# Recurrence lanes that count as emitted 300 instructions earlier, in a one-layer hybrid encoder step

## The chip, the cores and the metric

The kernel runs on one core of a Trainium2 chip. The metric is the device time of one execution in microseconds (us); lower is better. PE is TensorE's matmul stream and PEld its weight loads, DVE is VectorE, ACT ScalarE, POOL GpSimd, SP SyncE, which here only issues DMAs.

## The reference

One layer of a streaming encoder, for a prompt of 2048 frames and a sample of 32 frames with running state, model width 1024. All inputs are float32.

```python
h = _rmsnorm(x, attn_norm_g[l])
(u_a, qkv_b, qkv_c, z_c, a_c, b_c, q_d, k_d, v_d, g_d, gk_d) = _split_cols(einsum('btd,dc->btc', h, w_in[l]))
y_a, st_pool = _pool_mixer(u_a, ...)                 # trailing means over 2/4/8/16 frames, a 64x64 product
y_b = _band_attention_prompt(q_b, k_b, v_b, rel_bias[l])   # 4 heads, own chunk of 64 and the 8 before it
y_c, st_conv, st_d = _delta_mixer(qkv_c, z_c, a_c, b_c, ...)  # gated DeltaNet, chunks of 64, a state per head
y_d, st_g = _gla_mixer(q_d, k_d, v_d, g_d, gk_d, ...)      # gated linear attention, chunks of 64, a state per head
x = x + einsum('btc,cd->btd', concatenate([y_a, y_b, y_c, y_d]), w_out[l])
h2 = _rmsnorm(x, mlp_norm_g[l])
x = x + einsum('btf,fd->btd', square(relu(einsum('btd,df->btf', h2, w_up[l]))), w_down[l])
y = _rmsnorm(x, final_norm_g)
```

In DeltaNet each chunk of 64 frames solves a triangular system and then updates a 64x64 state per head; the next chunk needs that state. GLA likewise carries a 32x64 state per head from chunk to chunk. Attention has no such chain, but each head goes through scores, softmax, transposes and the product with the values.

## The kernel before

**Two phases.** Phase 1 (`phase1`) makes the mixer: the input projection, the four head groups and the output projection. Phase 2 (`phase2`) is the MLP in three blocks of 696 or 688 frames. Projections are split into a high and a low float32r part, so that each product is three matmuls (line 90 is the one line from which every matmul is recorded; line 94 records PE transposes).

**Phase 1 as a fill and three lanes.** The prompt is cut into four blocks of 512 frames. The *fill* is a generator: for each block `stage_in` projects the normed input piece by piece (tiles g on PE, weights `wt` split from `ldt` at lines 252 and 253, the input `hT` split at 255 and 256 or, for the output projection, 252 and 253) and spills the results to DRAM; after the four blocks `out_proj` loads the mixed rows (`yt`, line 1360) and the old x (`sg<-x_t`, line 1377) and adds the output projection to x (line 1421). Three *lanes* run beside it: delta (tiles d, un, X, Sd; `delta_tile`), attention (s, pT, oa, nb, qkr; `attn_head`, `attn`) and GLA (l, att, Qx, Cl; `gla`). A lane loads what the fill has spilled (qkr at line 734, nb at 713, lqke and qz at 1049 and 1052, ltk at 1055, lg at 1162) and writes its part of the mix with `mix_out` (transposes a on PE, a copy mo on ACT at line 848, a store). Small *jobs* are run by `tick`: stores, the pooling mix (a<-sg,pv on PE, line 670 on ACT), the norm of the next block (lines 311 and 321), and `delta_pre`, which inverts the triangular factors by 31 steps of two DVE instructions (tp at line 999, X at 1000) and transposes (ut at 1005, tr at 1007, then U at 1027).

**What sets the order.** `drive` emits the program: one step of the fill, now and then a tick of the jobs, and then from each lane as many steps as its rate has earned. What it emits is numbered; the scheduler of the framework then orders each engine's instructions by list scheduling: it keeps all dependences, follows a model of how long instructions take, and where several are ready for an engine it takes the one with the lowest number. `high_priority(offset=n)` lowers the numbers of what is emitted inside by n; phase 2 uses it with 400 for reads of its accumulators. Two things bind the fill to the lanes beyond data: `pace` puts the fill's next matmul behind what each lane had emitted on PE seven steps earlier, and accumulators, buffers and DRAM tiles are shared through pools (two accumulators `a`, one of each lane's, four loads `ldt`/`yt`, six `sg`, one nb, three qkr). Each engine runs its queue in order, and SP issues its DMAs in order.

Of the kernel before, what the change touches and what calls it, by code (L numbers as in the profile page):

```python
# [110 lines left out]
class K:  # L111
# [1317 lines left out]
    def drive(self, fill, lanes):  # L1429


        state = [[list(l), 0.0, None, 0] for l in lanes]
        live = True
        tk = 0.0
        hist, seen = [], {}
        while live:
            hist.append(dict(self.front))
            if fill is not None and len(hist) > LAG:
                past = hist[len(hist) - 1 - LAG]
                self.bound = [x for l, x in past.items() if seen.get(l) is not x]  # L1440
                seen = past
            w = next(fill, None) if fill is not None else None
            if w is None:
                fill = None
            tk += 2.6 if w is None else w
            if tk > 2.0:
                tk = 0.0
                self.tick()
            live = False
            for self.lane, st in enumerate(state):  # L1450
                work = st[0]
                if not work:
                    continue
                live = True
                cond, g, rate, _ = work[0]
                if self.rest:
                    if st[2] is None:
                        st[2] = (sum(w[3] for w in work) - st[3]) / self.rest
                    rate = max(rate, st[2])
                if not cond():  # L1460
                    st[1] = min(st[1], 0.5)
                    continue
                st[1] += (2.6 if w is None else w) * rate
                while st[1] >= 1.0 and work:
                    st[1] -= 1.0
                    st[3] += 1
                    if next(g, g) is g:
                        work.pop(0)
                        st[3] = 0
                        if not work or not work[0][0]():  # L1470
                            break
                        g = work[0][1]
            self.lane = None
        self.bound = []
# [490 lines left out]
```

## Time and profile before

| What | Before |
|---|---|
| device time, median of 3 runs | 2712.63 us (2703.66 to 2714.59) |
| the profiled execution: its own time, its span | 2714.24 us, 2712.5 us |
| PE, PEld busy | 2594.9 us (96%), 2415.3 us (89%) |
| DVE, ACT, POOL busy | 1962.2 us (72%), 1079.0 us (40%), 872.9 us (32%) |
| mean granted clock of TensorE | 0.98 |
| from 200 to 1300 us: PE, PEld, DVE busy | 1039.47, 890.66 and 820.24 of 1100 us |

The span reaches from the first to the last instruction of the profiled execution. PE's matmuls are pipelined and their ends are modelled, so a busy PE need not be at its peak. Phase 1 ends at about 1290 us. The granted clock is the share of 2.4 GHz; it has two levels, 1.0 and 0.5.

### The profile page before, as it was taken

The page shows a single profiled execution, that of the slowest core. Times are in us where ns is not written, and L with a number is a line of the kernel's source. Part 1 is how long each engine was busy: PE and PEld are TensorE (multiplying, and loading weights), DVE is VectorE, ACT ScalarE, POOL GpSimd, SP SyncE. Part 2 cuts the span into 40 slices and gives each one's busy share as a digit, 9 for nine tenths or more (in the row PEclk, how much of TensorE's full clock was granted, in tenths as well). Part 3 has the DMA queues.
Part 4 walks back from the last instruction along what each step waited for, and adds up shares of the span by engine and source line. Part 5 has one row for each costly group of instructions (what it writes and reads, how often), then busy time and mean ns, then how long its engine had stood idle before and what let it go on. Part 6 is the DMA issues. An engine that isn't in the chain of part 4 may idle for free.

```text
span 2712.5 us, 44728 instructions
## 1 busy us (share of the span) xinstructions
PE 2594.9 (96%) x17012; PEld 2415.3 (89%) x17012; DVE 1962.2 (72%) x3498; ACT 1079.0 (40%) x1934; POOL 872.9 (32%) x1064
## 2 busy tenths in 40 slices
PE   7899998999899999998999999999999999999998
PEld 7787787788778877878999999999999999999998
DVE  6567779878887865566787667778766677767665
ACT  6435643653465443343433223443232343333232
POOL 4433564464446543322221112222212213211211
PEclk9998999999999999999999999999999999999999
DMA  5655454454545566366353222455322235222221
GB/s 165 175 152 162 124 179 146 129 159 137 150 139 162 158 185 195 103 209 205 105 180 114 70 71 78 139 161 171 111 70 86 75 108 160 80 70 79 71 70 50
DMA packets 229144, 349.21 MB, mean 129 GB/s; under 512 B 52032, under 2 KB 152784, under 8 KB 228928
## 3 DMA queue, kind: packets, MB, share of 16 engines
q1 hardware_dynamic: 162384, 295.49, 36.1%
q10 hardware_dynamic: 66480, 50.78, 5.7%
q8 instruction: 134, 2.20, 0.3%
q14 instruction: 82, 0.67, 0.1%
q0 software_dynamic: 64, 0.08, 0.0%
HBM read 273.83 MB, written 73.56 MB: 128 GB/s over the span
## 4 chain that ended last, share of the span: by engine, by line
PE 47%; DVE 7%; DMA 4%; issue 2%; ACT 1%; POOL 1%; SPq 0%; DVEq 0%; ACTq 0%; POOLq 0%
PE d L90 23%; PE u L90 19%; PE g L90 3%; DVE wx L253 1%; DVE acc L1824 1%; DMA cbd<-cb 1%; DVE wt L253 1%; DMA ldt<-w_o 1%; DMA x2d<-sg 1%; DVE h2T L253 1%; DVE acc L1853 1%; DVE u L253 1%; PE l L90 0%; DMA cb<-cbd 0%; PE s L90 0%
## 5 line engine op out<-in xcount | busy, mean ns | idle before, releaser
L90 PE MATMUL d<-u,wt 128*128 128x348 f32 (+1 forms) x2400 | 629.9, 323 | 4.5 <-DVE acc L1824 3.7
L90 PE MATMUL d<-u,wx 128*128 128x348 f32 (+1 forms) x2208 | 600.6, 323 | 9.5 <-DVE acc L1824 9.4
L90 PE MATMUL g<-hT,wt 128*128 128x512 f32 (+2 forms) x2544 | 544.2, 362 | 18.3 <-DVE sg L1421 7.1
L1824 DVE TENSOR_TENSOR acc<-acc,d 128x348 f32<-128x348 f32 (+1 forms) x752 | 376.0, 510 | 214.3 <-PE d L90 206.5
L90 PE MATMUL u<-h2T,wt 128*128 128x348 f32 (+1 forms) x2024 | 515.9, 323 | 6.5 <-DVE wt L253 6.2
L90 PE MATMUL u<-h2T,wx 128*128 128x348 f32 (+1 forms) x2008 | 514.0, 323 | 1.1 <-ACT wt L252 0.9
L90 PEld LDWEIGHTS g<-hT,wt 128*128 128x128 f32 x2544 | 414.4, 194 | 81.1 <-DVE hT L256 6.1
L90 PEld LDWEIGHTS d<-u,wt 128*128 128x128 f32 x2400 | 426.6, 189 | 7.5 <-DVE acc L1824 5.3
L90 PEld LDWEIGHTS d<-u,wx 128*128 128x128 f32 x2208 | 396.7, 189 | 13.9 <-DVE acc L1824 13.1
L90 PEld LDWEIGHTS u<-h2T,wt 128*128 128x128 f32 x2024 | 357.7, 189 | 8.9 <-DVE wt L253 7.4
L90 PEld LDWEIGHTS u<-h2T,wx 128*128 128x128 f32 x2008 | 356.6, 190 | 2.7 <-ACT wt L252 1.1
L1699 POOL TENSOR_TENSOR s<-wur 128x512 f32<-128x512 f32 x48 | 74.4, 1550 | 725.3 <-DMA wur<-w_up 603.7
L90 PE MATMUL g<-wt,hT 128*128 128x256 f32 (+3 forms) x1632 | 243.7, 298 | 6.7 <-DVE sg L464 3.1
L90 PEld LDWEIGHTS g<-wt,hT 128*128 128x128 f32 (+1 forms) x1632 | 214.3, 189 | 16.0 <-DVE sg L464 4.1
L253 DVE TENSOR_TENSOR wt<-ldt,wt 128x1024 fp32r<-128x1024 f32 (+1 forms) x120 | 163.4, 1361 | 70.2 <-ACT wt L252 69.4
L252 ACT CAST wt<-wur 128x1024 fp32r<-128x1024 f32 x126 | 131.4, 1049 | 184.9 <-PE u L90 119.3
L252 ACT CAST wx<-wur 128x1024 fp32r<-128x1024 f32 x114 | 118.8, 1049 | 200.7 <-PE u L90 144.9
L1780 ACT COPY k<-u 128x348 f32<-128x348 f32 (+1 forms) x144 | 64.0, 447 | 281.6 <-PE u L90 280.8
L253 DVE TENSOR_TENSOR wx<-wur,wt 128x1024 fp32r<-128x1024 f32 x125 | 158.7, 1269 | 19.5 <-PE d L90 8.4
L252 ACT CAST wt<-ldt 128x1024 fp32r<-128x1024 f32 (+1 forms) x120 | 126.0, 1050 | 115.9 <-PE g L90 78.3
L1699 POOL TENSOR_TENSOR wur<-s,wur 128x512 f32<-128x512 f32 x48 | 66.4, 1383 | 324.7 <-DVE wt L253 172.2
L253 DVE TENSOR_TENSOR wt<-wur,wx 128x1024 fp32r<-128x1024 f32 x114 | 146.2, 1285 | 24.7 <-PE d L90 8.4
(348 smaller groups left out, 3821.8 us busy)
## 6 DMA issues: line engine op xcount, KB each, us to landing
wur<-w_up SPq DMA_DIRECT2D x96, 512.0 KB, 3.7
wur<-w_down SPq DMA_DIRECT2D x96, 512.0 KB, 4.2
ldt<-w_fm SPq DMA_DIRECT2D x56, 512.0 KB, 4.4
ldt<-w_o SPq DMA_DIRECT2D x32, 512.0 KB, 4.9
ldt<-w_tm SPq DMA_DIRECT2D x24, 512.0 KB, 4.2
fmd<-sg ACTq DMA_DIRECT2D x46, 256.0 KB, 2.9
qkr<-fmd SPq DMA_DIRECT2D x88, 128.0 KB, 3.5
tmd<-sg ACTq DMA_DIRECT2D x64, 128.0 KB, 2.6
```

The costliest lines, as they stand in the source:

```text
L90: return self.order(self.k.nc.tensor.matmul(out, lhsT, rhs, start=not have, stop=True, skip_group_check=True))
L252: nc.scalar.copy(hi, src)
L253: (eng or nc.vector).tensor_tensor(lo, src, hi.bitcast(F32), ALU.subtract)
L1699: add = lambda o, x, y: nc.gpsimd.tensor_tensor(o, x, y, ALU.add)
L1780: nc.scalar.copy(keep[n], ps[z].t[:, :h])
L1824: nc.vector.tensor_tensor(x, x, ps.t[:, :cw], ALU.add)
L1853: nc.vector.scalar_tensor_tensor(x, x, self.fg[:, i:i + 1], fs[0], ALU.mult, ALU.mult)
```

## The change

In `drive`, the step of a lane is emitted inside `high_priority(offset=300)`. All that a lane emits (its matmuls, its DVE, ACT and POOL instructions and its loads) is numbered as if it had been emitted 300 instructions earlier; what the fill and the jobs emit keeps its number, the stores of `mix_out` among it, since `tick` emits them. No instruction is added or taken away, and buffers and dependences stay.

```diff
                 while st[1] >= 1.0 and work:
                     st[1] -= 1.0
                     st[3] += 1
-                    if next(g, g) is g:
+                    with self.tc.high_priority(offset=300):
+                        end = next(g, g) is g
+                    if end:
                         work.pop(0)
                         st[3] = 0
                         if not work or not work[0][0]():
```

The built programs show where instructions went. Three places follow, each with the rows of before first; the numbers in names are those of the tiles, the same in both programs.

ACT, in the third block of the input projection: mo_7983 and mo_7988 are copies of two lanes' transposes for the mix, U_8195 belongs to `delta_pre`, sg_8133 to sg_8141 to the norm of the next block, sg_7859 to the pooling mix. Before:

```order
L697 COPY pT_7909<-s_334_7812 128x640
L252 CAST wt_8119<-ldt_8117 128x1024
L311 ACTIVATE sg_8133<-xt_8129 128x512
L311 ACTIVATE sg_8135<-xt_8129 128x512
L1027 ACTIVATE U_8195<-ut_8191,c_62 128x4x32
L848 COPY mo_7983<-a_342_7980 128x256
L165 DMA mixd0_143<-mo_7983 128x2x128
L670 ACTIVATE sg_7859<-a_345_8021,pv1_210 128x512
L311 ACTIVATE sg_8138<-xt_8130 128x512
L848 COPY mo_7988<-a_343_7985 128x256
L311 ACTIVATE sg_8141<-xt_8130 128x512
L165 DMA mixd0_143<-mo_7988 128x2x128
```

With the change:

```order
L252 CAST wt_8119<-ldt_8117 128x1024
L311 ACTIVATE sg_8133<-xt_8129 128x512
L311 ACTIVATE sg_8135<-xt_8129 128x512
L848 COPY mo_7983<-a_342_7980 128x256
L848 COPY mo_7988<-a_343_7985 128x256
L311 ACTIVATE sg_8138<-xt_8130 128x512
L165 DMA mixd0_143<-mo_7983 128x2x128
L165 DMA mixd0_143<-mo_7988 128x2x128
L670 ACTIVATE sg_7859<-a_345_8021,pv1_210 128x512
L687 ACTIVATE s_8084,st_8085<-s_8084,st_8085 128x640
L311 ACTIVATE sg_8141<-xt_8130 128x512
L1027 ACTIVATE U_8195<-ut_8191,c_62 128x4x32
```

The two copies now stand next to each other ahead of U_8195, which has moved behind the softmax instruction of line 687.

DVE, in the second block: att_4671 is the GLA lane's score tile, X32_4517 and tp_4520 belong to the inversion in `delta_pre`, wt_4923 is a weight, Sd_4653 the delta lane's state. Before:

```order
L1000 TENSOR_TENSOR X32_4517<-X32_4517,tp_4520 128x22x10
L253 TENSOR_TENSOR wt_4712<-ldt_4709,wt_4711 128x1024
L999 TENSOR_TENSOR tp_4520<-B_4515,X32_4517 128x231
L1265 COPY_PREDICATED att_4671<-gm_213,l_187_4673 128x256
L1000 TENSOR_TENSOR X32_4517<-X32_4517,tp_4520 128x21x11
L686 ISA s_4739,st_4740<-s_190_4736,nb_4411 128x256
L686 ISA st_4740 128x1
L1265 COPY_PREDICATED att_4671<-gm_213,l_187_4673 128x128x2
L999 TENSOR_TENSOR tp_4520<-B_4515,X32_4517 128x240
L253 TENSOR_TENSOR wt_4923<-ldt_4920,wt_4922 128x1024
L1117 TENSOR_TENSOR Sd_4653<-Sd_4653,a_192_4785 64x2x64 x2
L632 COPY uh_4912<-ua_4715 128x32
```

With the change:

```order
L663 SCALAR_TENSOR_TENSOR sg_4915<-sg_4915,c_62,ua_4715 128x512
L999 TENSOR_TENSOR tp_4520<-B_4515,X32_4517 128x247
L1000 TENSOR_TENSOR X32_4517<-X32_4517,tp_4520 128x19x13
L686 ISA s_4739,st_4740<-s_190_4736,nb_4411 128x256
L686 ISA st_4740 128x1
L834 TENSOR_REDUCE st_4797<-sqo_4796 128x4
L1265 COPY_PREDICATED att_4671<-gm_213,l_187_4673 128x256
L999 TENSOR_TENSOR tp_4520<-B_4515,X32_4517 128x252
L253 TENSOR_TENSOR wt_4923<-ldt_4920,wt_4922 128x1024
L1117 TENSOR_TENSOR Sd_4653<-Sd_4653,a_192_4785 64x2x64 x2
L632 COPY uh_4912<-ua_4715 128x32
L1265 COPY_PREDICATED att_4671<-gm_213,l_187_4673 128x128x2
```

The second att_4671 row (128x128x2) now has the later inversion steps, the reduction st_4797, the split of wt_4923, Sd_4653 and uh_4912 ahead of it.

SP, at the start of the output projection: yt_11485 is the last quarter of the mixed rows, sg_... the old x, ldt_... weights; nb_11313, qkr_... and qz_... are loads of the attention and delta lanes. Before (nb_11313 is the twelfth row):

```order
L1360 DMA yt_11485<-mixd0_143 128x2x512
L1052 DMA qz_113<-fmd0_139 128x2x64
L1377 DMA sg_11477<-x_t 128x512
L276 DMA ldt_11495<-w_o 128x1024
L1377 DMA sg_11507<-x_t 128x512
L276 DMA ldt_11501<-w_o 128x1024
L1377 DMA sg_11597<-x_t 128x512
L1377 DMA sg_11670<-x_t 128x512
L276 DMA ldt_11658<-w_o 128x1024
L1164 DMA lvg_11691<-tmd0_141 128x512
L1377 DMA sg_11777<-x_t 128x512
L713 DMA nb_11313<-bd_614 128x640
```

With the change:

```order
L1162 DMA lg_12051<-fmd0_139 128x384
L1164 DMA lvg_11691<-tmd0_141 128x512
L1049 DMA lqke_11797<-fmd0_139 128x256
L713 DMA nb_11313<-bd_614 128x640
L734 DMA qkr_11415<-fmd0_139 64x4x128 x2
L734 DMA qkr_11418<-fmd0_139 64x4x128 x2
L734 DMA qkr_11421<-fmd0_139 64x4x128 x2
L1052 DMA qz_114<-fmd0_139 128x2x64
L1377 DMA sg_11477<-x_t 128x512
L1360 DMA yt_11485<-mixd0_143 128x2x512
L276 DMA ldt_11495<-w_o 128x1024
L276 DMA ldt_11501<-w_o 128x1024
```

The loads nb_11313, six of qkr and qz_114 now stand ahead of sg_11477, yt_11485 and the first two weight loads; before, nb_11313 stood eleven rows behind yt_11485, and the qkr behind it.

## Rows read from the trace of the kernel before

**Rows 1.** The page, part 1: span, busy time and share of each engine.

```profile
span 2712.5 us, 44728 instructions
...
PE 2594.9 (96%) x17012; PEld 2415.3 (89%) x17012; DVE 1962.2 (72%) x3498; ACT 1079.0 (40%) x1934; POOL 872.9 (32%) x1064
```

**Rows 2.** Busy time by stretch; after the engines granted clock, DMA share, GB/s.

```profile
200.00:1300.00 1100.00, 1039.47 (x7220) 890.66 (x7219) 820.24 (x1720) 514.81 (x1036) 487.42 (x714) 0.97 0.52 158
1300.00:2700.00 1400.00, 1379.52 (x8557) 1367.45 (x8555) 1012.22 (x1499) 466.06 (x668) 297.60 (x205) 0.99 0.33 100
```

**Rows 3.** PE's waits, 200 to 1300 us: us in total, times, longest.

```profile
PE g L90 <- DVE sg L1421: 7.1, 5, 2.7
PE s L94 <- ACT s L687: 5.6, 9, 1.6
PE l L90 <- DVE att L1265: 5.0, 5, 1.8
...
PE a L90 <- ACT mo L848: 3.9, 2, 3.5
...
PE s L90 <- ACT pT L697: 2.7, 5, 1.1
```

**Rows 4.** Timeline (start, duration, in brackets idle before), and busy time, 699 to 706 us.

```profile
700.38 1.23 DVE L1005 STREAM_TRANSPOSE ut<-X 128x1024 f32<-128x1024 f32 x1
701.54 1.88 DVE L1007 STREAM_TRANSPOSE tr<-X 128x1024 f32<-128x1024 f32 x1
701.65 0.54 ACT L1027 ACTIVATE U<-ut,c 128x128 f32<-128x128 f32 x1 [5.11 <-DVE ut L1005]
702.06 0.37 ACT L848 COPY mo<-a 128x256 f32<-128x256 f32 x1
702.49 2.07 PE L90 MATMUL a<-sg,pv 128*128 128x512 f32 x2 [3.53 <-ACT mo L848]
703.34 0.25 DVE L702 TENSOR_SCALAR oa<-s,st 128x64 f32<-128x64 f32 x1
704.03 1.59 DVE L321 TENSOR_TENSOR sg<-sg 128x512 f32<-128x512 f32 x1
699.00:706.00 7.00, 3.35 (x7) 1.76 (x7) 7.00 (x7) 2.13 (x5) 4.37 (x6) 0.51 0.96 260
```

**Rows 5.** Timeline of PE, 954 to 965 us.

```profile
955.24 1.10 PE L90 MATMUL l<-Qx,Cl 128*128 128x256 f32 x4 [1.13 <-DVE att L1265]
961.48 1.64 PE L90 MATMUL l<-lvg,att 128*128 128x64 f32 x8 [1.79 <-DVE att L1265]
```

**Rows 6.** Timeline of PE and DVE near 410 us, and busy time by stretch.

```profile
410.89 1.13 PE L90 MATMUL l<-Qx,Cl 128*128 128x256 f32 x4 [0.73 <-DVE att L1265]
410.64 0.43 DVE L999 TENSOR_TENSOR tp<-B,X 128x240 f32<-128x240 f32 x1
415.72 0.41 DVE L999 TENSOR_TENSOR tp<-B,X 128x252 f32<-128x252 f32 x1
300.00:400.00 100.00, 100.00 (x716) 85.26 (x716) 75.16 (x188) 48.12 (x112) 59.98 (x98) 1.00 0.59 177
400.00:420.00 20.00, 19.15 (x144) 17.24 (x143) 19.52 (x47) 5.60 (x14) 9.09 (x15) 1.00 0.28 89
```

**Rows 7.** Timeline of SP, DVE and PE, 994 to 1014 us.

```profile
994.92 0.37 SPq L1360 DMA_DIRECT2D yt<-mixd  x1
1005.07 0.35 SPq L713 DMA_DIRECT2D nb<-bd  x1
1005.61 2.00 SPq L734 DMA_DIRECT2D qkr<-fmd  x2
1009.38 2.57 SPq L734 DMA_DIRECT2D qkr<-fmd  x4
1001.26 3.29 DVE L253 TENSOR_TENSOR hT<-yt,hT 128x1024 fp32r<-128x1024 f32 x1
1003.28 3.01 PE L90 MATMUL g<-hT,wt 128*128 128x512 f32 x12
```

## Prediction

> **What bounds the kernel now.** I read the page first: of the span of 2712.5 us TensorE (PE) is busy for 2594.9 us, so no order of instructions that keeps the work can give back more than its idle 117.6 us by filling gaps [rows 1]. Then I cut the span into the stretch ahead of the change's reach, the stretch it reaches and the rest. The built order of the changed kernel is, on PE, the same as before up to its row 1009 (a projection matmul that ran at about 176 us) and again from its row 6515 on (about 1,243 us); on VectorE (DVE), ScalarE (ACT) and GpSimd (POOL) the first and last differences lie in about the same stretch. So the MLP, 1300 us onwards, keeps its order, and only the stretch from 200 to 1300 us matters. There PE is busy 1039.47 of 1100 us: 60.5 us are idle [rows 2]. The granted clock is 0.97 in it; 3% of 1100 us is 33 us spent at the half rate beyond what full rate would need, as far as work was waiting [rows 2]. Both together, some 94 us or 3.4% of the span, are all that a better order could find there. The reader should see next that the idle time is in crumbs: the largest group of PE's waits is 7.1 us in five pieces, and the releasers are DVE and ACT instructions of lanes and of the projection alike [rows 3]. No single wait is worth the 0.5% (13.6 us) which I take as the least that can be told from no change.
>
> **The change part by part.** It adds and removes no instruction. It moves lane instructions ahead of instructions of the fill and of the background jobs when both are ready for one engine. Between PE rows 1009 and 6514 another instruction stands in 3,407 of 5,506 places, but only 1,504 moved by ten places or more, and on DVE 105 did. Ten matmuls are about 1.5 us (1039.47 us over 7,220 matmuls is 144 ns for one). So most of the move is jitter of a few us, and its worth has to be read at places.
>
> *Place A, a gain, at 702 us.* PE sits idle for 3.53 us ahead of the pooling matmul a<-sg,pv, until ACT has copied mo<-a and so freed the accumulator. The copy took 0.37 us; it stood in ACT's queue behind U<-ut, which waited 5.11 us for a transpose on DVE [rows 4]. In the change both mo copies stand ahead of U<-ut. What is late next is oa<-s,st on DVE, which PE needs for its next transposes: it ended at 703.59 us, behind the transposes ut (1.23 us) and tr (1.88 us) [rows 4]. The change puts it ahead of those two, and a 1.59 us addition of the norm ahead of it: 1.5 us sooner. The stall therefore shrinks by 0 at least and 3.53 at most; I take 2 us, a little over the 1.5. The stretch from 699 to 706 us ran at a clock of 0.51 with PE busy 3.35 of 7 us [rows 4]; without the stall that work could go at up to twice the rate, 1.7 us more. I take half, 0.8 us.
> By the Trainium skill, page "TensorE: Matmul & The Clock Gate", section "Why this matters for your kernels", gaps between bursts of matmuls bring the half rate back, so that a stall is paid twice. The trace agrees here, with the 0.51; by the rule all of the 1.7 us would come back, and the sum below would be 0.9 us lower.
>
> *More gains of the same kind.* Two stalls of 1.13 and 1.79 us at 955 and 961 us wait for att of the GLA lane, which stood behind steps of the 32x32 inversion on DVE [rows 5]. In the change the first att copy stands ahead of two steps more, and two more projection matmuls stand ahead of the second stall's instruction. Together 2.9 us at most and 0 at least; I take half, 1.5 us.
>
> *Place B, a loss, at 410 us.* PE's l<-Qx,Cl waits 0.73 us for the copy att on DVE. In the change nine instructions that came after this copy stand ahead of it: steps of the inversion, a weight split, a state update and a reduction, 4.85 us by their durations here (the first and the last of the nine are in [rows 6]); the PE instruction stays where it was, 0.25 us of matmuls aside. DVE is busy for 19.52 of 20 us there, so there is little idle time to swallow it locally; but from 300 to 400 us it was busy for 75.16 of 100 [rows 6], and the same steps may then run earlier. So 0 to 4.85 us; I take half, 2.4 us.
>
> *Place C, the loads, at 995 us.* SP issues its DMAs in order. Before, the last quarter of the mixer output, yt, went out at 994.92 us, ahead of the next head's bias nb (1005.07 us) and its six qkr loads (issued from 1005.61 to 1011.95 us) [rows 7]. In the change yt, x_t and two weight loads stand behind nb, all six qkr and one qz. Those are lane loads that wait for lane buffers. If the lane frees its buffers no sooner, yt goes out at 1011.95 us, 17.0 us later; if it frees them as much sooner as the delta lane's matmuls there move up (up to 16 us by the matmuls now behind them), it goes out hardly later. DVE's split of yt ended at 1004.55 us and PE's projection run at 1003.28 us followed without a wait [rows 7], so lateness here is soon a stall. Bounds 0 and 17.0 us. The lane's attention copies move up by some 7 us of ACT work, and lane matmuls are put in front of the projection in the same place; I take 2 us, near the lower end.
>
> *The sum.* Gains 2 + 0.8 + 1.5 = 4.3 us; losses 2.4 + 2 = 4.4 us. The stalls I did not follow, about 50 of the 60.5 us, lie on both sides of such exchanges; I count their balance as 0 and their spread as some 10 us. The sum is +0.1 us on the profiled execution's own 2714.24 us (span 2712.5 and 1.7 around it), which is 1.6 us over the runs' median of 2712.63; set against that median, 2712 us.
>
> **The rivals.**
> *Faster, 2696 us.* The lanes, being recurrences, are the latency chains; put first, their own stalls vanish. The waits of PE for lane products are s 5.6, att 5.0, mo 3.9 and pT 2.7, together 17.2 us [rows 3], and with them perhaps half of the 33 us of lost clock, 16 us: 33 us if all goes well (2679 us), and half of it, some 17 us, as a likely size. For it: places A and 955 us. Against it: these stalls are 3.5 us at most and a queue that lets one through early makes another late, as at B.
> *Faster for another reason, about 2700 us.* In this stretch matmuls of the lanes and of the projection overlap differently when they alternate differently, and PEld (weight loads) is busy for 890.66 of 1100 us, where the MLP has 1367.45 of 1400 [rows 2]. If 5% of the 209 us that PEld is short of 1100 came back, that is 10 us. It stays within what I call the same.
> The Trainium skill, page "Perfetto Trace Analysis", section "Identifying the Most-Contended Engine", says that matmul busy time misjudges headroom because matmuls are pipelined, and that LDWEIGHTS busy time is the better sign. By it the room in this stretch is 209 us, not 60.5. The rows show the two shares apart, as the page says they can be; no row shows that order alone closes it.
> *Slower, 2729 us.* Place C at its full price: in-order SP holds yt, x_t and w_o behind lane loads, the projection starts 17.0 us late, and PE has no lane work left to fill in. It decides from the point where yt lands after about 1,003 us, that is where qkr goes out later than some 999 us.
> *Nothing moves that matters.* The jitter stays inside the slack; 2713 us, the same class as the forecast.
>
> **How the numbers follow.** Forecast (exchanges that cancel) 0.46; nothing that matters 0.09; the larger faster rival 0.22 and a part of the smaller, 0.02, beyond 0.5%; the slower rival 0.16 and unseen late loads or stalls of its kind 0.05. So faster 0.24, same 0.55, slower 0.21. The predicted time is 2712 us. Alone, the likeliest case spans 2702 to 2723 us. The range that leaves 2 in 10 out takes in both rivals' centres and what lies half as far again beyond them: 2688 to 2736 us.
>
> **What would show it.** Right: the order differs only up to 1,243 us and the MLP lasts as long as before; PE's idle time from 200 to 1300 us stays within 50 to 72 us; the 3.53 us wait for mo is under 2 us; a wait for att or un of a few us stands near 410 us. C is right at its lower end if yt goes out before 1,000 us or the projection's first run shows no wait over 3 us. Wrong: a single new PE wait over 8 us, or a stretch 200 to 1300 us that ends 14 us sooner or later.

## The result and the profile after

The changed kernel took 2722.53 us (median of 10 runs, 2718.36 to 2728.64) against 2711.03 us (10 runs, 2703.66 to 2714.59): a ratio of 1.0054, 95% interval 1.0043 to 1.0065. The medians lie 11.5 us apart; the ratio, which is not that of the two medians, stands for 14.6 us. It is slower where no change was forecast: no change lies outside the interval, the 0.5% bound inside it. The time lies inside the stated range.

The page's first part of the changed kernel answers to [rows 1], and the two stretches (columns as there) to [rows 2]:

```profile
PE 2612.0 (96%) x17012; PEld 2424.9 (89%) x17012; DVE 1963.4 (72%) x3498; ACT 1081.6 (40%) x1934; POOL 875.9 (32%) x1064
```

```profile
200.00:1300.00 1100.00, 1045.26 (x7144) 890.25 (x7143) 810.53 (x1705) 509.77 (x1025) 486.97 (x713) 0.97 0.51 157
1300.00:2700.00 1400.00, 1378.02 (x8553) 1364.46 (x8552) 1014.68 (x1494) 470.86 (x672) 298.54 (x204) 0.99 0.33 101
```

The MLP is as busy as before (1378.02 against 1379.52 us). The span grew by 10.1 us (2722.6 against 2712.5), and it did not grow by waiting: PE's idle time fell by 7.0 us, from 117.6 to 110.6, while its busy time rose by 17.1 us, from 2594.9 to 2612.0, for the same 17012 matmul records. In the stretch from 200 to 1300 us the count tells the same: 7,144 matmul records instead of 7,220, in more busy time. A reader who looks for the loss among the waits alone looks in the wrong column. Work at the half clock takes longer and counts as busy too (the four records of `l<-Qx,Cl` near 410 us took 1.13 us before at a clock of 1.00 [rows 6], and 2.08 us in the changed kernel at 0.64); its share comes with the experiments. The waits of PE from 200 to 1300 us, largest first, are again crumbs, as in [rows 3]:

```profile
PE g L90 <- DVE hT L256: 5.9, 7, 2.6
PE s L94 <- ACT s L687: 4.6, 7, 1.6
PE a L90 <- ACT sg L449: 4.5, 5, 2.3
PE l L90 <- DVE att L1265: 4.2, 3, 1.9
PE a L94 <- DVE oa L702: 3.8, 2, 3.5
...
PE s L90 <- DVE oa L702: 3.3, 3, 1.6
...
PE s L90 <- ACT pT L697: 2.2, 3, 1.0
```

**Where the busy time came from.** The delta lane issues its small matmuls in groups: four on 64x64 parts of the array (`a<-lc`, `d<-X,ltk`, `a<-un,ltk`, `d<-un,ltk`), eight on 32x32 parts (`a<-tr,at`, `a<-ut,px`); each instruction leaves two records. Groups of PE instructions by tile, 150 to 1290 us, before the change (the count, then busy time in us, mean ns of one, then idle time ahead of them):

```profile
L90 PE MATMUL d<-X,ltk 64*64 64x64 f32 (+1 forms) x264 | 23.7, 225 | 0.1
L90 PE MATMUL d<-un,ltk 64*64 64x64 f32 (+1 forms) x264 | 22.6, 223 | 1.6 <-DVE un L1108 1.6
L90 PE MATMUL a<-lc 64*64 64x128 f32 (+1 forms) x200 | 16.7, 279 | 0.0
L90 PE MATMUL a<-un,ltk 64*64 64x64 f32 (+1 forms) x264 | 14.8, 230 | 0.6 <-DVE sqo L1282 0.6
L90 PE MATMUL a<-ut,px 32*32 32x32 f32 x256 | 10.5, 228 | 3.3 <-ACT sg L670 1.8 <-DVE px L1025 1.4
L90 PE MATMUL a<-tr,at 32*32 32x32 f32 x256 | 10.4, 228 | 3.6 <-DVE tr L1007 2.0 <-DVE sqo L1282 1.0 <-ACT mo L848 0.3
```

and in the changed kernel:

```profile
L90 PE MATMUL d<-un,ltk 64*64 64x64 f32 (+1 forms) x264 | 25.1, 228 | 1.5 <-DVE un L1108 1.5
L90 PE MATMUL d<-X,ltk 64*64 64x64 f32 (+1 forms) x264 | 22.8, 224 | 0.0
L90 PE MATMUL a<-lc 64*64 64x128 f32 (+1 forms) x200 | 20.6, 280 | 0.0
L90 PE MATMUL a<-un,ltk 64*64 64x64 f32 (+1 forms) x264 | 15.9, 231 | 0.0
L90 PE MATMUL a<-tr,at 32*32 32x32 f32 x256 | 12.8, 227 | 2.1 <-DVE tr L1007 2.0
L90 PE MATMUL a<-ut,px 32*32 32x32 f32 x256 | 12.0, 227 | 3.1 <-ACT sg L670 1.7 <-DVE px L1025 1.4
```

The six rows add up to 98.7 us before and 109.2 after: 10.5 us more for equal counts, while the mean duration of one hardly moves (279 and 280 ns, 228 and 227). Busy time of a row counts an instant once, so what was lost is overlap: fewer of them run at the same time. (Different rows overlap too, so microseconds of these rows are not all microseconds of PE's whole busy time.) The timeline of PE shows how. Before, near 348 us, two groups in a row:

```profile
347.88 0.66 PE L90 MATMUL a<-lc 64*64 64x128 f32 x8
348.47 0.44 PE L94 MATMUL a<-c,lc 128*128 128x128 f32 x2
348.84 0.66 PE L90 MATMUL a<-lc 64*64 64x128 f32 x8
```

and in the changed kernel a group that is cut by a transpose of the attention lane:

```profile
341.21 0.66 PE L90 MATMUL a<-lc 64*64 64x128 f32 x8
342.17 0.65 PE L90 MATMUL a<-lc 64*64 64x128 f32 x4
342.75 0.33 PE L94 MATMUL s<-c,s 128*128 128x128 f32 x1
343.01 0.65 PE L90 MATMUL a<-lc 64*64 64x128 f32 x4
```

Eight records take 0.66 us together, four take 0.65 alone. Half a group costs as much as a whole one. Behind these rows, the trace's single records of the whole group start in four pairs, 0.013 us apart within a pair and 0.11 to 0.16 us from pair to pair; those of the half start one by one, 0.11 to 0.16 us apart. By the Trainium skill, page "TensorEngine Tiling (Array Packing)", section "Key Properties", separate parts of the array work independently; these rows agree, with the 0.66 for eight and the 0.65 for four. The Trainium skill says in the same place that a switch of the tiling mode drains the engine; no row here shows what that costs by itself.

The built order of the change has 47 cuts (one to eleven other matmuls stand between two of a group) in 34 groups, that of the kernel before 15 in 14; the column "cut" below counts cuts. The ones that cut are other lanes' matmuls in most cases, `s<-c,s` first. Row by row the busy time follows the cuts: `a<-lc` 0 to 8 cuts, 3.9 us more; `d<-un,ltk` 5 to 13, 2.5 more; `a<-tr,at` 2 to 12, 2.4 more; `a<-ut,px` 1 to 8, 1.5 more; `a<-un,ltk` 0 to 3, 1.1 more; and `d<-X,ltk`, cut less often (7 to 3), 0.9 less.

**Place B** added its share. Timeline of PE and DVE near 410 us in the changed kernel, and busy time by 5 us:

```profile
409.94 0.44 PE L94 MATMUL s<-c,s 128*128 128x128 f32 x2 [1.44 <-ACT s L687]
412.33 0.72 DVE L1265 COPY_PREDICATED att<-gm,l 128x256 f32<-128x256 uint8 x1
412.86 0.20 DVE L688 RECIPROCAL st<-st 128x1 f32<-128x1 f32 x1
413.11 2.08 PE L90 MATMUL l<-Qx,Cl 128*128 128x256 f32 x4 [2.73 <-DVE st L688]
```

```profile
405.00:410.00 5.00, 3.56 (x34) 3.13 (x33) 4.97 (x9) 1.85 (x6) 3.19 (x3) 1.00 0.30 105
410.00:415.00 5.00, 2.27 (x7) 1.68 (x8) 4.65 (x12) 0.66 (x3) 1.34 (x2) 0.64 0.44 139
415.00:420.00 5.00, 5.00 (x32) 5.00 (x31) 2.97 (x9) 0.00 (x0) 0.00 (x0) 0.68 0.16 45
```

Two waits of 1.44 and 2.73 us stand where 0.73 us stood [rows 6], behind them the clock is 0.64 and 0.68 (part of the time at the lower level, 1.2 GHz), and DVE is nearly full (4.97 and 4.65 of 5 us) while PE waits.

### The profile page after: what moved, and what is told of

Same layout as the page of the kernel before. It is cut to its first block, busy times and chain, and to the rows that moved or that the text cites. A ratio compares the mean times of both kernels' runs of the same rounds, so it can differ in the third digit from the quotient of the medians.

```text
span 2722.6 us, 44706 instructions
## 1 busy us (share of the span) xinstructions
PE 2612.0 (96%) x17012; PEld 2424.9 (89%) x17012; DVE 1963.4 (72%) x3498; ACT 1081.6 (40%) x1934; POOL 875.9 (32%) x1064
## 4 chain that ended last, share of the span: by engine, by line
PE 47%; DVE 6%; DMA 3%; issue 2%; ACT 1%; POOL 1%; SPq 0%; DVEq 0%; ACTq 0%; POOLq 0%
PE d L90 24%; PE u L90 19%; PE g L90 2%; DVE wt L253 1%; DVE acc L1826 1%; DVE wx L253 1%; DVE h2T L253 1%; DMA ldt<-w_o 1%; DVE acc L1855 1%; DMA cb<-cbd 1%; PE s L90 0%; DMA cbd<-cb 0%; PE l L90 0%; DMA cb<-x2d 0%; POOL wur L1701 0%
## 5 line engine op out<-in xcount | busy, mean ns | idle before, releaser
L90 PE MATMUL g<-hT,wt 128*128 128x512 f32 (+2 forms) x2544 | 537.8, 360 | 17.7 <-DVE hT L256 5.9
L90 PE MATMUL g<-wt,hT 128*128 128x256 f32 (+3 forms) x1632 | 249.8, 303 | 6.8 <-DVE sg L464 2.7
L90 PEld LDWEIGHTS g<-wt,hT 128*128 128x128 f32 (+1 forms) x1632 | 220.0, 194 | 17.4 <-issue 3.9
```

The lines of the kernel that those rows point to most:

```text
L90: return self.order(self.k.nc.tensor.matmul(out, lhsT, rhs, start=not have, stop=True, skip_group_check=True))
```

## The experiments

Theory G says that the loss is PE's own time, by cut groups. Theory S says it is stalls and the half clock behind them. Later theories are named where they come up. The new order that an edit of the numbers brings about is called a deal. Each run was timed in five rounds beside the kernel before on the same chip (medians of before: 2702.33 us for the first four, 2704.53 for the next four, 2703.63 for the last four). The table has the ratio to before, the cuts in the built order, the busy time of the six groups above (150 to 1290 us), PE's busy and idle time over the whole span of the profiled run, and the half clock: time times one minus the granted clock, mean over all runs of the kernel, less the same for before in the same call. Three limits of the table: the kernel before, timed against itself (e12), shows +2.0 of half clock, so differences of that size say nothing; its first profile was taken where its median was 2711.03 us, so that idle times are better compared with e12; and the profiled executions of e7 and e10 were the fastest of their kernels, 6 and 10 us under the median.

```
run                ratio  95% interval    cut  six groups  PE busy  PE idle  half clock
before                                     15     98.7     2594.9   117.6
change             1.0054 1.0043-1.0065    47    109.2     2612.0   110.6
e1_whole_after     1.0026 1.0013-1.0039     0     95.9     2594.9   115.7     +5.0
e2_whole_before    1.0015 1.0006-1.0025     0     95.7     2584.7   117.1     -0.5
e3_cut_before      1.0038 1.0023-1.0053    75    111.7     2603.2   110.5     -1.3
e4_offset4         1.0005 0.9996-1.0014    36    103.4     2596.2   110.1     -2.5
e5_offset0         1.0039 1.0023-1.0055    36    103.2     2598.8   113.1     +2.9
e6_raise_only      1.0035 1.0021-1.0050    24    103.6     2601.2   111.0     +1.3
e7_raise_whole     0.9971 0.9960-0.9982     0     96.4     2582.5   109.0     -1.0
e8_change_again    1.0057 1.0043-1.0071    47    109.2     2614.6   107.6     +8.2
e9_whole200        0.9984 0.9969-0.9999     0     95.6     2588.7   112.2     +1.7
e10_whole450       1.0032 1.0015-1.0048     0     95.7     2584.1   118.3     +5.1
e11_raise450       1.0083 1.0062-1.0105    18    101.2     2608.0   117.8    +18.1
e12_before_again   0.9994 0.9980-1.0008    15     99.4     2594.2   110.5     +2.0
```

**Groups held whole in the change (e1).** `PT.mm` gets a flag, and the second and later matmuls of a group carry it:

```diff
-    def mm(self, out, r0, m, lhsT, rhs, bank=0):
+    def mm(self, out, r0, m, lhsT, rhs, bank=0, tail=False):
+        if tail:
+            with self.k.tc.high_priority(offset=3000):
+                return self.mm(out, r0, m, lhsT, rhs, bank)
...
-                px.mm(pxv[ch, 1, h], co, cs, U[ch, h, :cs], X[ch, h])
+                px.mm(pxv[ch, 1, h], co, cs, U[ch, h, :cs], X[ch, h], tail=bool(h))
```

> The changed kernel, in which the second and later matmuls of each group of small matmuls of the delta lane (four on 64x64 parts of the array, eight on 32x32 parts) count as emitted 3000 instructions further up, so that nothing is put into a group once its first matmul is out: in the built order 0 groups are cut by one to eleven other matmuls, against 47 in the changed kernel and 15 in the one before. Theory G (the loss is PE's own time: cut groups lose the overlap of their small matmuls, some 0.25 us a cut, 8.1 us for 32 cuts more): the time of these matmuls falls by about 12 us against the changed kernel and the whole to 2711 us, give or take 6 for stalls that are dealt anew. Theory S (the loss is stalls as at 410 us and the half clock behind them; PE's own time does not depend on the order): within 4 us of the changed kernel's 2722 us.

Measured: 1.0026 where the change has 1.0054 and 1.0057, so some 8 us come back (give or take some 5, by the intervals), less than the 11 that G expected but inside its margin. S alone is out: it had PE's own time independent of the order, and the six rows fell by 13.3 us. It is not out as a part: with no group cut 0.26%, some 7 us, of loss remains, the half clock is still 5.0 us over that of before, and one wait at place B still stands (2.8 us, as it does in e7 below). The six rows add up to 95.9 us; three of them, back at or under the values of before:

```profile
L93 PE MATMUL a<-lc 64*64 64x128 f32 (+1 forms) x200 | 16.7, 279 | 0.0
L93 PE MATMUL a<-ut,px 32*32 32x32 f32 x256 | 10.3, 228 | 1.1 <-ACT sg L673 1.1
L93 PE MATMUL a<-tr,at 32*32 32x32 f32 x256 | 10.0, 227 | 3.2 <-DVE tr L1010 3.1
```

**The same in the kernel before (e2).** The edit of e1 on the kernel before.

> The same holding together of the groups in the kernel before: 0 cut groups against 15. Theory G: PE's time in these matmuls falls by about 4 us, the whole is 2707 us, give or take 6 for stalls dealt anew. Theory S: 2711 us, give or take 6, with no change in the time of the small matmuls.

The groups fell by 3.0 us (98.7 to 95.7), as G said, but the whole became 0.15% slower, not faster, and lies where S had it. The small hold changes 2,077 places of PE's order, and what that dealt elsewhere cost more than the groups gave; the profiled execution has 117.1 us of PE idle time against 110.5 in e12. G sizes its own term, not the whole.

**Groups cut by an edit in the kernel before (e3).** The flag stands on the second half of a group, and moves it down:

```diff
+            with self.k.tc.high_priority(offset=-40):
+                return self.mm(out, r0, m, lhsT, rhs, bank)
...
+                px.mm(pxv[ch, 1, h], co, cs, U[ch, h, :cs], X[ch, h], tail=h >= 2)
```

> The kernel before, in which the second half of each such group counts as emitted 40 instructions further down, so that other matmuls come between: 75 cut groups against 15. Theory G: 60 cuts more at 0.25 us are 15 us in the time of the small matmuls; the whole is about 2726 us, slower than the changed kernel. Theory S: no lane runs earlier, the stalls stay about as they were, 2711 us give or take 6.

No lane is raised, and the kernel is 0.38% slower: the groups' time rose by 13.0 us (98.7 to 111.7), 0.22 us a cut, and the whole by about 10, less than the 15 that G expected. (Ten more cuts, with more than eleven matmuls inside, are not in the 75; with them it is 0.19 us a cut.) PE's whole busy time rose by 8.3 us, its idle time is that of e12 (110.5 us), and the half clock is no higher: the loss is not the later half stalling the lane. S expected no change. Cuts, with no lane raised, make a loss of 0.38% where the change has 0.54 to 0.57%.

**A raise of next to nothing (e4).**

```diff
-                    with self.tc.high_priority(offset=300):
+                    with self.tc.high_priority(offset=4):
```

> The change with an offset of 4 instructions in place of 300: the lanes gain next to nothing in rank, but the order is dealt anew (2,594 of PE's 15,428 places differ from before, 692 by ten or more) and 36 groups are cut. Theory G: 21 cuts more at 0.25 us, about 5 us slower than before, 2716 us. Theory S in its form that raised lanes make the fill late: next to no change, 2711 us. A third reading, that any new deal of this order loses because the one before was a lucky one: as slow as the changed kernel, 2722 us.

The groups took 4.7 us more (103.4), as G had it, but the whole is the same as before within 0.14%, as S had it. The half clock is 2.5 us lower, which would pay for half of it but hardly stands out of the noise; the other half is open. The reading that any new deal loses as much as the change is out.

**No raise at all (e5).** The same line with `offset=0`. What made this run worth while is a second effect of the two lines, which the section on the change does not tell: on leaving, the guard sets the counter of the numbers back to where it was. In the built program two lane steps that follow each other held the numbers 4155 to 4162 and 4155 to 4161, where without the guard the second would go on from the first. Lanes then share numbers, and the scheduler alternates between them.

> The change with an offset of 0: nothing is raised, but the guard around a lane's step still sets the counter of the numbers back when it is left, so that what is emitted next gets the same numbers again. Steps of several lanes that follow each other, and the fill's step behind them, then hold equal numbers. 36 small groups are cut, against 15 before and 47 in the change; 2,296 of PE's places differ from before. Theory N (half of the change's loss comes from this giving back of the numbers, by way of cut groups): PE's own time at full clock rises by 3 to 7 us (21 cuts at 0.14 to 0.32 us), the whole by about 5 us, 0.2%. Theory R (the raise by 300 is what costs): the time of the kernel before within 0.1%.

0.39% slower with nothing raised: R is wrong, and N is right in kind but too low. The groups took 4.5 us of some 10, and only the three rows that hold the 36 cuts rose (`d<-un,ltk`, `d<-X,ltk`, `a<-un,ltk`); the uncut three took no longer than before. Of the other 6 us, up to 2.9 are half clock; the rest was not found.

**The raise alone (e6).** The counter moves on as if the guard were not there; with an offset of 0 this builds the order of before exactly.

```diff
                     with self.tc.high_priority(offset=300):
+                        at = self.tc.cur_priority
                         end = next(g, g) is g
+                        at = self.tc.cur_priority - at
+                    self.tc.cur_priority += at
```

> The raise by 300 alone: behind each lane step the counter is moved on by as many numbers as the step has used, so that every lane instruction counts as emitted 300 instructions further up and no number is used twice by following steps. 24 small groups are cut. Theory N with cut groups: 9 cuts more than before, 1 to 3 us of PE's own time, and the whole is up to 0.2% slower than before. Theory R: as slow as the change, some 0.5% over before.

0.35% slower, between the two theories (0.2 and 0.5%). The groups took 4.9 us more for 9 cuts more (103.6), so a cut is no fixed price; `a<-lc` alone, cut 5 times, took 19.4 us instead of 16.7, 0.54 us a cut. Raising and giving back the numbers each cost about 0.37%, and both together 0.57%, less than their sum.

**The raise alone with the groups held (e7).** The edits of e6 and of e1, the latter with the counter moved on by one behind each held matmul.

> The raise by 300 alone, and the second and later matmuls of each small group raised by 3000 more, with the counter moved on in both: 0 cut groups. Cut groups as the cause: PE's own time 1 to 2 us under the kernel before, and the whole within 0.2% of before, on either side by how the stalls fall. Theory R: some 0.5% slower.

The fastest version: 0.9971, some 8 us under before by the ratio (5 by the medians), more than the 0.2% forecast, and 24 us under the change; R is wrong again. Against e6 only the hold is new; it took 7.2 us from the groups and 17 us from the whole, so 10 us came from elsewhere in the new order. The first part of its page, and its stretch from 200 to 1300 us:

```profile
PE 2582.5 (96%) x17012; PEld 2409.8 (90%) x17012; DVE 1965.6 (73%) x3498; ACT 1081.0 (40%) x1934; POOL 875.3 (33%) x1064
```

```profile
200.00:1300.00 1100.00, 1045.26 (x7298) 903.57 (x7299) 832.49 (x1731) 521.11 (x1041) 487.75 (x717) 0.98 0.51 159
```

PE is busy for 1045.26 us of this stretch both in the change and here, and the records of matmuls there are 7,144 in the change and 7,298 in this one.

**The change and the kernel before once more (e8, e12).**

> The change as it is, beside the others on this chip: 0.5% slower than before again, with PE's own time at full clock some 10 us above that of before; where the idle time and the time at half clock differ from its first profile, the difference is the spread of single executions.

> The kernel before as it is, for its profile on this chip: ratio 1.000 within 0.1%. PE's own time at full clock in the mixer is that of its first profile within 1 us, if it is a property of the order; its idle time within 3 us and its time at half clock within some 6 us, the spread of single executions.

The times came as expected, and so did the groups' time; the idle time spread more than the 3 us expected. The groups' busy time is a property of the order: 109.2 and 109.2 us for the change, 98.7 and 99.4 for before. The idle time of single executions of before differs by 7 us (117.6 and 110.5), and that bounds what idle time of one profile can say (from 200 to 1300 us the two differ by 3.0 us, 60.5 and 57.5).

**Other raises with the groups held, and without (e9, e10, e11).** The edits of e7 with 200 and 450, and that of e6 with 450.

> As the run with the raise alone and the groups held whole, but raised by 200 in place of 300: another deal of the order, 0 cut groups. Theory W (a raise gains a few us of idle time as long as no group is cut): PE's own time at full clock 2 to 4 us under the kernel before, idle time a few us lower, the whole 0.1 to 0.4% faster than before. Theory L (0.9971 at 300 was a lucky deal): anywhere from 0.3% faster to 0.3% slower.

> The same with 450 in place of 300, 0 cut groups. Theory W: 0.1 to 0.4% faster than before again. Theory L: anywhere from 0.3% faster to 0.3% slower.

> The raise by 450 alone, numbers moved on, groups not held: 18 cut groups against 15 before. Cut groups as the cause: 3 cuts more, PE's time in the small matmuls within 1.5 us of before, and the whole within 0.2% of before, slower than the run with the groups held by some 5 us (18 cuts at 0.25 to 0.3 us). If the raise itself costs: 0.3% slower or more, like the raise by 300.

At 200 the gain is 0.16%, at 450 it is a loss of 0.32%: theory W (a raise gains as long as no group is cut) falls, and the 0.9971 at 300 is in part the luck of a deal. At 450 without the hold the loss is 0.83% with only 18 cuts and 2.5 us in the groups, where cuts as the cause would have given 0.2% at most; here the loss lies where S put it. The half clock is 18.1 us more than before's, and PE's idle time 7.3 us more than in e12. Two of its stretches of 20 us have a clock of 0.74, from 455 and from 490 us; the second lies where a new block's projection starts. e11's waits of PE from 450 to 515 us, and its stretch from 490 to 510 us:

```profile
PE g L90 <- DVE hT L256: 3.8, 2, 2.0
PE l L90 <- DVE att L1265: 3.0, 1, 3.0
PE g L90 <- ACT hT L255: 1.5, 1, 1.5
```

```profile
490.00:510.00 20.00, 14.05 (x83) 12.58 (x82) 19.30 (x32) 12.22 (x31) 6.31 (x8) 0.74 0.40 122
```

The projection waits for its staged activations hT, and 6 of 20 us are idle, with a clock of 0.74; the kernel before, profiled again, had PE busy for 17.82 us there at 1.00. What holds hT back at 450 was not settled. The hold takes 14 us out of this kernel (1.0083 to 1.0032), more than the groups' 5.5 us.

## Why the prediction was wrong

*The step that failed* is in the part on the change: "It adds and removes no instruction ... So most of the move is jitter of a few us, and its worth has to be read at places." From this the sum took PE's work as the same 144 ns a matmul in any order and looked for gains and losses among the waits only. But the time that small matmuls take on PE depends on their neighbours: cut groups lose their overlap. That term was 0 in the sum; it is 10.5 us in the six groups' rows, 8 us of time when it is taken back in e1, and some 10 us where cuts are put in and no lane is raised (e3). It is not the whole of the loss: some 7 us stay in e1. The only term of half clock in the sum was the 0.8 us gained at place A; in the change it is 8.2 us a run more than before (e8), 5.0 of them left in e1.

*The numbers given back* were missed too. The prediction counted the two lines as a raise by 300. They do a second thing, which costs 0.39% without any raise (e5).

*The idle time* was forecast well: 50 to 72 us from 200 to 1300 us, and 1100 less 1045.26 is 54.7; before it was 60.5 (53.5 and 57.5 in the second executions, e8 and e12). The four waits that the first rival named did shrink, from 17.2 to 11.0 us, and the waits for `oa` rose from 1.5 to 7.1 us. So the objection that the prediction set against this rival, that a queue which lets one through early makes another late, is what happened. None of the signs set for being wrong came true (a new wait over 8 us, a stretch 14 us longer); all of them looked at waits or totals, and none at busy time.

*Place A* was mis-sized: 2 us of gain and 0.8 of clock were taken, and it is nothing. The wait for `mo` is gone, but the next one named, `oa`, came as late as `mo` had been. Timeline of DVE and PE, and busy time from 705 to 712 us, in the changed kernel:

```profile
706.48 0.27 DVE L702 TENSOR_SCALAR oa<-s,st 128x64 f32<-128x64 f32 x1
706.80 0.47 PE L94 MATMUL a<-c,oa 128*128 128x128 f32 x1 [3.49 <-DVE oa L702]
```

```profile
705.00:712.00 7.00, 5.20 (x13) 3.71 (x14) 6.97 (x13) 2.75 (x6) 3.70 (x5) 0.52 0.53 158
```

3.49 us instead of 3.53, at a clock of 0.52 instead of 0.51 [rows 4]. DVE is full here (6.97 of 7 us), and `oa` stood behind other DVE work; moving the copies on ACT did not help. The "right" sign that was set, a wait for `mo` under 2 us, was met and meant nothing.

*The stalls near 955 us* went from 1.13 and 1.79 us [rows 5] to one of 1.7: 1.2 us gained where 1.5 was taken.

*Place B* was right in place, sign and size for the wait that it named: `l<-Qx,Cl` waited 2.73 us instead of 0.73, 2.0 us more where 2.4 was taken. The profile names `st` as what ended it, but `att`, which the prediction named, ended 0.01 us earlier (413.05 and 413.06). Two things were missed: the 1.44 us in front of the transpose `s<-c,s`, and the half clock behind both. In the 10 us from 410 the clock is 0.66 on the mean, which is 3.4 us of full speed lost at most; in the second execution, with the same two waits, it is 0.83 over 10 us, 1.7 us.

*Place C* was right at its lower end. The loads stand in the forecast order, the six qkr ahead of yt:

```profile
1009.97 4.77 SPq L734 DMA_DIRECT2D qkr<-fmd  x6
1016.27 0.37 SPq L1360 DMA_DIRECT2D yt<-mixd  x1
```

Both rows are SP's timeline in the changed kernel. yt left 21 us later than before (994.92 us, [rows 7]), of which some part is the lateness of the whole kernel by then, yet PE's waits for hT from 1000 to 1035 us come to 1.2 us in three pieces. The slower rival named this place and was wrong about it; slower came from elsewhere.

*The rival on overlap* named the right mechanism, matmuls that overlap differently when they alternate differently, with the wrong sign and the wrong meter. In e3, where cuts are all that was put in, PEld's busy time fell by 3.2 us over the span (2415.3 to 2412.1) while PE's rose by 8.3. In the change PEld's is the same from 200 to 1300 us (890.66 and 890.25 us, for 76 records fewer) and 9.6 us higher over the span. The rival looked at lane against projection; in the change most matmuls that cut were another lane's.

*What stays open.* The half clock: 8.2 us more in the change (58.5 us a run over 6 runs against 50.3 over 27), of which only place B's part was traced to a stall; how far the groups' time sets the whole, since the hold took 3.0, 13.3, 7.2 and 5.5 us from the groups in its four pairs of runs (before and e2, the change and e1, e6 and e7, e11 and e10) and changed the whole by +4, -8, -17 and -14 us; and why new deals with no cut group end between 0.29% under and 0.32% over before. A run that mends place B alone was not made, since each edit of the numbers deals the whole order anew.

## What to carry to other kernels

Before a change of order is costed by its waits, look whether the bound engine's own work depends on the order: compare "busy" of a group with count times mean, and where it is far less (here 16.7 us against 200 times 279 ns, 55.8 us), the group lives on overlap that a neighbour can break. Hold such groups together (the first member at its own rank, the others right behind it) before ranks are changed, and measure the result: the raise by 300 lost 0.35% without the hold and gained 0.29% with it, that by 450 lost 0.83% and 0.32%, and in the kernel before the hold alone lost 0.15%. A guard that lends a rank may also hand back the numbers it used; test it with an offset of 0.

## What the runs showed that was not expected

Four small matmul records on 64x64 parts alone last as long as eight (0.65 and 0.66 us), and a cut costs 0.22 us on the mean in e3 (13.0 us for 60 more cuts), 0.33 us in the change (10.5 us for 32). An order with no raise at all, by shared numbers alone, costs 0.39%. The busy time of the six groups came out the same within 0.7 us in two executions of one kernel, while PE's idle time differed by 7 us.
